# Two transformer blocks on one core: TensorE operands at chosen byte offsets

## Chip, cores and metric

The kernel runs on one core of a Trainium2 chip. The metric is the device time of one execution in microseconds (us); lower is better. Before the change the median of 3 runs is 2297.12 us (2294.67 to 2298.26).

## The reference

256 tokens of width 1024 pass through two blocks, all in float32. What matters here is the chain of matrix products:

```
first_block, 2 layers:  proj = rmsnorm(x) @ w_in            # 1024 -> queries, keys, values, gates
                        three attention branches -> ya, yb, yc
                        merged = sum_b sigmoid(m_g[b]) * (y_b @ w_br_b)
                        x = x + merged @ w_out
second_block, 2 layers (a latent and a context sequence, 256 tokens each):
    x, ctx = half_ffn(x), half_ffn(ctx)     # (silu(h @ w_gate) * (h @ w_up)) @ w_down, 1024 -> 2816 -> 1024
    layer 0: Fourier mixing of both, @ four_w       layer 1: retention, 4 heads, of the latent reading ctx
    x = half_ffn(x); in layer 0 also ctx = half_ffn(ctx)
return rmsnorm(x)
```

## The kernel before

Every product is made exact enough for float32 by splitting each operand into a rounded part and a rest (`wh` and `wl` for weights; `hh`/`ho`, `ah`/`ao`, `xh`/`xo`, `yh`/`yo`, `mh`/`mo`, `gh`/`go`, `qh`/`qo`, `kh`/`ko`, `vh`/`vo`, `Sh`/`So`, `zh`/`zo`, `dh`/`dl` for the rest) and adding three matmuls, in `mm3` (L489 to L491) or written out. A matmul here has a stationary operand of 128 columns, loaded by an instruction of its own, and a moving operand of 256, 384, 452 or 512 columns; both are float32 and lie in SBUF, so a slice of 512 columns takes 2048 bytes of a partition.

The weights come in one long stream. `Stream` loads tiles of up to 2048 columns (`raw`, 3 buffers), and ACT (L388) and DVE (L389) split them into `wh` and `wl`, 4 buffers of 4096 bytes each. The order of all work is written out by hand, and side work (attention, sums for the modulation, norms) is put between the matmuls by `th.tick()`.

The stages, in order, with the operands that matter:

- `layer(0)`, `layer(1)`: projections with `wh`/`wl` moving (512, 452, 384 columns) and `xh`/`xo` stationary (L640 to L642); gates with `xh`/`xo` moving (256); branch products with `wh`/`wl` moving and `yh`/`yo` stationary (L1186 to L1188); the output product with `mh`/`mo` moving (256).
- `ffn(0,0)`, `ffn(0,2)`, `ffn(1,0)` work on both sequences at once (`lanes` 2): gate and up products with `hh`/`ho` moving (512), down products with `ah`/`ao` moving (512). The first two column blocks of gate and up (`start`) and the last two of down (`tail`) go one sequence at a time, with 256 columns.
- `fourier()` between the first two: two transforms with `dh`/`dl` moving (256) and `hh`/`ho`, then `zh`/`zo` stationary, then a product with `hh`/`ho` moving (256).
- `retention()`: per head `rq` (`hh` moving, 256), `rk` (`hh` moving, 512), `rv` and `rg` (`wh`/`wl` moving, 512, `hh`/`ho` stationary, L1598 to L1600), attention (`Sh`/`So` stationary, `vh`/`vo` moving, 512; `kh`/`ko` stationary, `qh`/`qo` moving, 256), and at the end `ro` (`gh`/`go` moving, 256).
- `ffn(1,2)` works on the latent alone (`lanes` 1): `hh`/`ho` and `ah`/`ao` moving, 256 columns.

Where a tile lies follows from its pool. Pools are stacked; within one, tiles lie one behind the other in the order in which they are asked for, each with its size rounded up to 32 bytes. Most pools grow from the lower end. The pools `b2` (`hh`, `ho`, `ss2`, `Rb`, ..., `r4`, `r1`, and small buffers) and `xc` grow downward from the upper end, so that a larger tile in `b2` moves all tiles of `b2` that were asked for before it, and `xc`, to lower addresses. `wh`, `wl`, `xh`, `xo`, `yh`, `yo`, `dh`, `dl` begin at multiples of 256 bytes. Slices of 512 bytes (128 columns), 1024 and 2048 bytes keep a tile's offset within 256 bytes, so that one number describes all slices of a tile.

Of the kernel before, what the change touches and what calls it, by code (L numbers as in the profile page):

```python
# [21 lines left out]
F32 = mybir.dt.float32  # L22
F32R = mybir.dt.float32r
# [7 lines left out]
D, T, KB = 1024, 256, 8  # L31
# [4 lines left out]
RAW, UNIT = 2048, 1024  # L36


# ---------------------------------------------------------------- order of the weights

def xs_items(key, n):
    return [(key, 4 * n, [(0, 2 * n), (2 * n, 4 * n)])] * 2
# [106 lines left out]
    }  # L149


# ---------------------------------------------------------------- layout on the host

def qk_columns():
    def heads(n, ids):
# [170 lines left out]
            "dft": dft_tab(), "decay": decay_tab()}  # L326


# ---------------------------------------------------------------- the program

class Stream:
    AHEAD = 2
# [113 lines left out]
def build(tc, aps, stage=99):  # L446
    nc = tc.nc
    pe, act, dve, pool = nc.tensor, nc.scalar, nc.vector, nc.gpsimd
    from contextlib import ExitStack
    ctx = ExitStack()  # L450
    with ctx:
# [38 lines left out]
            pe.matmul(out, wh, xlo, start=False, stop=False)  # L490
            pe.matmul(out, wl, xh, start=False, stop=last)  # L491

        # ---- adaLN
        def on_ada(key, item):
            _, l, i, n = key
            th.spawn(ada_sum(l, i, n, item))
# [95 lines left out]
                dve.scalar_tensor_tensor(sc[:, :, 0:2], ct.rearrange(kc, c=2), 1.0, ch.rearrange(kc, c=2),  # L592
                                         op0=OP.add, op1=OP.mult)

        # ================================================================ first block
        FB = ctx.enter_context(ExitStack())
        fp = FB.enter_context(tc.tile_pool(name="fb", bufs=1, reuse_waits="tile"))
        xh = fp.tile([128, KB, T], F32R, name="xh")
# [48 lines left out]
        Z = {}  # L647
# [81 lines left out]
        def open_second():  # L729
            ctx.enter_context(B2)  # L730
            ctx.enter_context(XC)
            bp = Z["bp"] = B2.enter_context(tc.tile_pool(name="b2", bufs=1, side=OTHER_SIDE, reuse_waits="tile"))
            xcp = XC.enter_context(tc.tile_pool(name="xc", bufs=1, side=OTHER_SIDE, reuse_waits="tile"))
            xc = xcp.tile([128, KB, T], F32, name="xc")
            nc.scalar.dma_start(xc.rearrange("p k t -> p (k t)"), aps["ctxt"])
            Z["x"] = [xl, xc]
            Z["hh"] = bp.tile([128, KB, 512], F32R, name="hh")
            Z["ho"] = bp.tile([128, KB, 512], F32R, name="ho")
            Z["ss"] = bp.tile([128, 512], F32, name="ss2")
            Z["Rb"] = bp.tile([128, 512], F32, name="Rb")  # L740
            Z["ss1"] = bp.tile([128, T], F32, name="ss1", tag="s1")
            Z["sp"] = bp.tile([128, 2, 3, KB, 2], F32, name="sp")
            Z["sp1"] = bp.tile([128, KB], F32, name="sp1")
            Z["gx"] = bp.tile([128, 2, 3, KB, 2], F32, name="gx")
            Z["r"] = bp.tile([128, 4], F32, name="r4")
            Z["r1"] = bp.tile([128, 2], F32, name="r1")
            th.spawn(ctx_thread(), 2)

# [100 lines left out]
        def layer(l):  # L849
# [83 lines left out]
                pe.matmul(out, qk[hb:hb + 64, qs // 2, t * 128:(t + 1) * 128], qk[hb:hb + 64, ks // 2, 0:L],  # L933
                          start=True, stop=True)

            # ---- the index of branch b
            def index_thread():
                while ("qk", 2) not in flags:
                    yield 1
# [34 lines left out]
                    dve.tensor_tensor(outs[t], outs[t], cms[t], op=OP.add)  # L974
                    flags.add(("bm", t))

            # ---- softmax attention, as a chain of jobs
            jobs = []
            for t in range(2):
                m = (mask0 if t == 0 else mask1)(0)  # L980
# [170 lines left out]
            AT.close()  # L1151
            MT = ExitStack()
            mp = MT.enter_context(tc.tile_pool(name=f"mrg{l}", bufs=1, reuse_waits="tile"))
            mg = mp.tile([128, 2, 1024], F32, name="mg")
            mh = mp.tile([128, KB, T], F32R, name="mh")
            mo = mp.tile([128, KB, T], F32R, name="mo")
# [54 lines left out]
            for q in range(2):  # L1211
                ps = [bank("pj") for _ in range(4)]
                for kh in range(2):
                    for u in range(2):
                        wh, wl = W.get(("out", l, q, kh))
                        for i in range(2):
# [5 lines left out]
                            if kh == 1:  # L1222
                                b = 4 * q + m
# [27 lines left out]
        for l in range(2):  # L1251
            layer(l)
        FB.close()

        # ================================================================ second block
        def ffn(l, j, lanes, nxt, first=0, ready=(), on_k=None, first_s=None, post=None):
            N = 256 * lanes
            FF = ExitStack()
            qp = FF.enter_context(tc.tile_pool(name=f"ffn{l}{j}", bufs=1, reuse_waits="tile"))
            hh, ho, gx = Z["hh"], Z["ho"], Z["gx"]  # L1260
            ah = qp.tile([128, 11, N], F32R, name="ah")
            ao = qp.tile([128, 11, N], F32R, name="ao")
# [121 lines left out]
        def dft_open():  # L1384
            dp = DF.enter_context(tc.tile_pool(name="dft", bufs=1, reuse_waits="tile"))
            Z["dh"] = dp.tile([128, 3, 2, 256], F32R, name="dh")
            Z["dl"] = dp.tile([128, 3, 2, 256], F32R, name="dl")
            def parts():
                yield 4
                for i in range(3):  # L1390
                    r = dp.tile([128, 512], F32, name="dr", tag="dr", bufs=1)
                    nc.sync.dma_start(r, aps["dft"][:, i * 512:(i + 1) * 512])
                    yield 3
                    fl = "p b c -> p (b c)"
                    h, l = Z["dh"][:, i].rearrange(fl), Z["dl"][:, i].rearrange(fl)
                    act.copy(h, r)
                    dve.tensor_tensor(l, r, h.bitcast(F32), op=OP.subtract)

                while not state.get("ada03"):
                    yield 1  # L1400
                f8 = dp.tile([128, 2, 2, 4, 2], F32R, name="f8")
                m = mods[:, 0, 24:32, :].rearrange("p (g d) r -> p d g r", d=2)
                for d in range(2):
                    act.copy(f8[:, 0, d], m[:, d])
                    dve.tensor_tensor(f8[:, 1, d], m[:, d], f8[:, 0, d].bitcast(F32), op=OP.subtract)
                yield 2
                ps = bank("at", "pf8")
                i = 0
                for d in range(2):
                    for x, t in ((0, Z["dh"]), (0, Z["dl"]), (1, Z["dh"])):  # L1410
                        pe.matmul(ps[0:8, 0:256], f8[:, x, d].rearrange("p g r -> p (g r)"), t[:, 0, d, :],
                                  start=(i == 0), stop=(i == 5))
                        i += 1
                yield 1
                c8 = dp.tile([8, 256], F32, name="c8")
                act.copy(c8, ps[0:8, 0:256])
                yield 2
                pt = bank("at", "pc8")
                for t in range(2):
                    pe.transpose(pt[:, 8 * t:8 * t + 8], c8[:, t * 128:(t + 1) * 128], ident[0:8, 0:8])  # L1420
                yield 1
                cm = Z["cm"] = dp.tile([128, 2, 4, 2], F32, name="cm")
                for t in range(2):
                    dve.tensor_copy(cm[:, t].rearrange("p g r -> p (g r)"), pt[:, 0:8])
                dve.tensor_copy(cm[0:1, 1].rearrange("p g r -> p (g r)"), pt[0:1, 8:16])

            th.spawn(parts())
# [7 lines left out]
        def fourier():  # L1435
# [1 line left out]
            xs = Z["x"]  # L1437
            FO = ExitStack()
            qp = FO.enter_context(tc.tile_pool(name="four", bufs=1, reuse_waits="tile"))
            pm = qp.tile([128, 2], F32, name="pm")  # L1440
            dve.memset(pm[:, 0:1], 1.0)
            dve.memset(pm[:, 1:2], -1.0)
            dve.memset(pm[0:1, :], 0.0)
            hh, ho = Z["hh"], Z["ho"]
# [3 lines left out]
            for a in range(2):  # L1448
                for g in range(4):
# [11 lines left out]
                    for t in range(2):  # L1461
                        o, r = ps[:, t * 256:(t + 1) * 256], Z["r"][:, 2 * a + t:2 * a + t + 1]
# [79 lines left out]
        def retention():  # L1542
            hh, ho, gx = Z["hh"], Z["ho"], Z["gx"]
# [3 lines left out]
            RC = ExitStack()  # L1547
            G2 = {}
            axl = qp.tile([128, 2, T], F32, name="axl")
            lg = qp.tile([128, 8], F32, name="lg")  # L1550
            nc.scalar.dma_start(axl.rearrange("p a t -> p (a t)"), aps["axial"])
            dve.tensor_scalar(lg, sm("decay"), -1.0, None, op0=OP.mult)
            dve.tensor_tensor(lg, lg, sm("decay"), op=OP.min)
# [50 lines left out]
            def att(h, qh, qo, kh, ko, vh, vo, sg):  # L1604
# [17 lines left out]
                for it in range(2):  # L1622
                    ps = bank("at", "pY")
                    ts = slice(it * 128, (it + 1) * 128)
                    for jt in range(4):
                        pe.matmul(ps, Sh[:, jt, ts], vh[:, jt, :], start=(jt == 0), stop=False)
                        pe.matmul(ps, Sh[:, jt, ts], vo[:, jt, :], start=False, stop=False)
                        pe.matmul(ps, So[:, jt, ts], vh[:, jt, :], start=False, stop=(jt == 3))
                    st = qp.tile([128, 16], F32, name="st", tag="st", bufs=2)
                    dve.bn_stats(st[:, 0:6], ps)  # L1630
                    dve.bn_aggr(st[:, 8:10], st[:, 0:6])
                    dve.tensor_scalar(st[:, 10:11], st[:, 9:10], 1.0, 1e-6, op0=OP.mult, op1=OP.add)
                    pool.tensor_tensor(st[:, 11:12], st[:, 10:11], mhalf[:, 0:1], op=OP.pow)
                    yn = qp.tile([128, 512], F32, name="yn", tag="tm", bufs=3)
                    dve.tensor_scalar(yn, ps, st[:, 8:9], st[:, 11:12], op0=OP.subtract, op1=OP.mult)
                    dve.tensor_tensor(yn, yn, sg[:, it, :], op=OP.mult)
                    yield 2
                    pt = bank("at", "pYt")
                    for b in range(4):
                        pe.transpose(pt[:, b * 128:(b + 1) * 128], yn[:, b * 128:(b + 1) * 128], ident)  # L1640
                    o = (slice(None), slice(4 * h, 4 * h + 4), ts)
                    pv = pt.rearrange("p (b t) -> p b t", t=128)
                    act.copy(G2["h"][o], pv)
                    dve.tensor_tensor(G2["o"][o], pv, G2["h"][o].bitcast(F32), op=OP.subtract)
# [164 lines left out]
```

## Time and profile before

| | |
|---|---|
| median of 3 runs | 2297.12 us |
| span of the profiled execution, first to last instruction | 2290.2 us |
| median less that span | 6.9 us |
| TensorE matmuls | 12576, busy 2254.1 us (98%) |
| TensorE weight loads | busy 1911.1 us (83%) |
| DVE / ACT / POOL busy | 62% / 40% / 8% |

The profile shows one execution. Matmuls overlap in it: the next one starts before the last has ended, so the time that a matmul costs in a dense stretch is the distance from its start to the next start (called its pace here), not its own length. That the pace is steady in a stretch is seen by dividing the time between two starts by the number of matmuls between them.

### The profile page before, as it was taken

To read this page: it belongs to the slowest core of one execution; us is meant where nothing else is said; L and a number is where in the kernel's file an instruction comes from. 1 tells how busy PE (TensorE), PEld (TensorE's weight loads), DVE (VectorE), ACT (ScalarE), POOL (GpSimd) and SP (SyncE) were. 2 spreads that over 40 slices of the span, in tenths; PEclk is the share of its full clock that TensorE was granted. 3 is DMA by queue.
4 is the path that set the end of the run, shared out by engine and by line. 5 is a ranking of instruction groups with operands and counts; after the bars stand their busy time and mean duration, and the time that the engine had idled before them with its cause. 6 is when DMAs were issued, how large, how long until landed. Compare 5 with 4: busy or idle time off the path is not lost.

```text
span 2290.2 us, 30969 instructions
## 1 busy us (share of the span) xinstructions
PE 2254.1 (98%) x12576; PEld 1911.1 (83%) x12576; DVE 1429.2 (62%) x2160; ACT 918.8 (40%) x1453; POOL 178.2 (8%) x204
## 2 busy tenths in 40 slices
PE   8999999999999999999999999999999999999998
PEld 7787887878877777898788778878878888899998
DVE  6776667766667666556666566555555656665554
ACT  5455544556432233455322324332232533335443
POOL 2100111012100000121000003000001100001001
PEclk9999999999999999999999999999999999999999
DMA  6344565444344544222445443334434423344553
GB/s 236 138 139 154 177 234 196 168 160 175 131 175 165 214 164 135 99 74 101 164 168 184 166 149 137 129 130 165 147 123 147 149 106 125 122 169 151 176 195 108
DMA packets 57167, 351.67 MB, mean 154 GB/s; under 512 B 6464, under 2 KB 6976, under 8 KB 23872
## 3 DMA queue, kind: packets, MB, share of 16 engines
q1 hardware_dynamic: 55872, 346.02, 42.6%
q10 hardware_dynamic: 1152, 3.67, 0.4%
q8 instruction: 98, 1.61, 0.3%
q14 instruction: 45, 0.37, 0.0%
HBM read 348.62 MB, written 1.05 MB: 153 GB/s over the span
## 4 chain that ended last, share of the span: by engine, by line
PE 86%; DVE 6%; ACT 3%; issue 3%; DMA 1%; POOL 1%; SPq 0%; DVEq 0%; ACTq 0%; POOLq 0%
PE pj L489 20%; PE pj L490 20%; PE pj L491 20%; PE pj L640 4%; PE pj L641 3%; PE pj L642 3%; DVE wl L389 2%; PE pj L1600 1%; PE pj L1599 1%; PE pj L1598 1%; ACT wh L388 1%; PE psc L933 1%; PE ada L527 1%; PE ppv L1061 1%; DMA raw<-w 1%
## 5 line engine op out<-in xcount | busy, mean ns | idle before, releaser
L389 DVE TENSOR_TENSOR wl<-raw,wh 128x1024 fp32r<-128x1024 f32 (+4 forms) x549 | 621.4, 1144 | 335.1 <-ACT wh L388 333.9
L388 ACT CAST wh<-raw 128x1024 fp32r<-128x1024 f32 (+4 forms) x549 | 520.6, 967 | 232.7 <-DMA raw<-w 149.7
L489 PE MATMUL pj<-hh,wh 128*128 128x512 f32 (+1 forms) x1632 | 573.1, 351 | 2.0 <-ACT hh L722 1.9
L490 PE MATMUL pj<-ho,wh 128*128 128x512 f32 (+1 forms) x1632 | 571.1, 350 | 3.1 <-POOL ho L727 1.6
L491 PE MATMUL pj<-hh,wl 128*128 128x512 f32 (+1 forms) x1632 | 570.0, 349 | 0.8 <-DVE wl L389 0.8
L489 PEld LDWEIGHTS pj<-hh,wh 128*128 128x128 f32 x1632 | 309.3, 189 | 52.2 <-ACT sg L1266 5.0
L490 PEld LDWEIGHTS pj<-ho,wh 128*128 128x128 f32 x1632 | 309.2, 189 | 46.9 <-POOL ho L727 2.8
L491 PEld LDWEIGHTS pj<-hh,wl 128*128 128x128 f32 x1632 | 309.0, 189 | 43.6 <-DVE wl L389 1.1
L516 DVE SCALAR_TENSOR_TENSOR acc<-raw,sc,acc 128x1024 f32<-128x1024 f32 x224 | 278.9, 1286 | 0.0
L489 PE MATMUL pj<-ah,wh 128*128 128x512 f32 (+1 forms) x770 | 269.6, 350 | 0.5 <-ACT wh L388 0.5
L491 PE MATMUL pj<-ah,wl 128*128 128x512 f32 (+1 forms) x770 | 267.8, 348 | 0.5 <-DVE wl L389 0.5
L490 PE MATMUL pj<-ao,wh 128*128 128x512 f32 (+1 forms) x770 | 267.7, 348 | 0.0
L640 PE MATMUL pj<-wh,xh 128*128 128x512 f32 (+2 forms) x480 | 191.0, 398 | 0.4 <-ACT wh L388 0.4
L641 PE MATMUL pj<-wl,xh 128*128 128x512 f32 (+2 forms) x480 | 184.1, 383 | 2.9 <-DVE wl L389 2.9
L642 PE MATMUL pj<-wh,xo 128*128 128x512 f32 (+2 forms) x480 | 183.2, 382 | 0.0
L1272 ACT CAST ah<-av 128x512 fp32r<-128x512 f32 (+1 forms) x88 | 49.9, 567 | 323.2 <-DVE av L1271 323.2
L489 PEld LDWEIGHTS pj<-ah,wh 128*128 128x128 f32 x770 | 145.6, 189 | 25.2 <-ACT wh L388 3.2
L491 PEld LDWEIGHTS pj<-ah,wl 128*128 128x128 f32 x770 | 145.6, 189 | 19.9 <-DVE wl L389 0.7
L490 PEld LDWEIGHTS pj<-ao,wh 128*128 128x128 f32 x770 | 145.7, 189 | 18.6
L1271 DVE TENSOR_TENSOR av<-sg,pj 128x512 f32<-128x512 f32 (+1 forms) x88 | 54.6, 621 | 161.3 <-PE pj L491 146.7
L670 POOL TENSOR_TENSOR ss<-ss,sq 128x256 f32<-128x256 f32 x55 | 48.6, 890 | 1328.9 <-ACT sq L668 1328.7
L1266 ACT ACTIVATE sg<-pj 128x512 f32<-128x512 f32 (+1 forms) x88 | 47.9, 544 | 206.6 <-PE pj L491 206.6
(304 smaller groups left out, 2964.3 us busy)
## 6 DMA issues: line engine op xcount, KB each, us to landing
raw<-w SPq DMA_DIRECT2D x258, 1024.0 KB, 4.8
raw<-w SPq DMA_DIRECT2D x64, 704.0 KB, 4.1
raw<-w SPq DMA_DIRECT2D x16, 768.0 KB, 4.2
de<-decay SPq DMA_DIRECT2D x24, 256.0 KB, 4.3
raw<-w SPq DMA_DIRECT2D x4, 904.0 KB, 4.5
raw<-w SPq DMA_DIRECT2D x6, 512.0 KB, 4.3
mk<-masks ACTq DMA_DIRECT2D x2, 768.0 KB, 5.6
xl<-xt SPq DMA_DIRECT2D x4, 256.0 KB, 5.5
```

The source lines that it names most:

```text
L388: self.nc.scalar.copy(hi[:, d], r[:, o])
L389: (sub or self.nc.vector).tensor_tensor(lo[:, d], r[:, o], hi[:, d].bitcast(F32), op=OP.subtract)
L489: pe.matmul(out, wh, xh, start=first, stop=False)
L490: pe.matmul(out, wh, xlo, start=False, stop=False)
L491: pe.matmul(out, wl, xh, start=False, stop=last)
L516: dve.scalar_tensor_tensor(acc[:, r, :], w, s, acc[:, r, :], op0=OP.mult, op1=OP.add)
L640: pe.matmul(o, xh[:, k, ts], wh[:, s], start=(k == 0), stop=False)
L641: pe.matmul(o, xh[:, k, ts], wl[:, s], start=False, stop=False)
L642: pe.matmul(o, xo[:, k, ts], wh[:, s], start=False, stop=(k == KB - 1))
L670: (dve if k == KB - 2 else pool).tensor_tensor(d, d, q, op=OP.add)
L1271: dve.tensor_tensor(av, sg, pu[:, :N], op=OP.mult)
L1272: act.copy(ah[:, m, :], av)
```

## The change

The change alters sizes of tiles, so that other tiles move, and in one place gives an operand a tile of its own. Nothing that is computed changes. The diff, without lines that only drop comments:

```diff
             Z["gx"] = bp.tile([128, 2, 3, KB, 2], F32, name="gx")
-            Z["r"] = bp.tile([128, 4], F32, name="r4")
+            Z["r"] = bp.tile([128, 36], F32, name="r4")
...
             mp = MT.enter_context(tc.tile_pool(name=f"mrg{l}", bufs=1, reuse_waits="tile"))
+            skew = mp.tile([128, (32, 40)[l]], F32, name="skew")
+            pool.memset(skew, 0.0)
             mg = mp.tile([128, 2, 1024], F32, name="mg")
...
             qp = FF.enter_context(tc.tile_pool(name=f"ffn{l}{j}", bufs=1, reuse_waits="tile"))
+            if lanes == 1:
+                skew = qp.tile([128, 48], F32, name="skew")
+                pool.memset(skew, 0.0)
+                Z["hh"] = qp.tile([128, KB, N], F32R, name="h1")
+                Z["ho"] = qp.tile([128, KB, N], F32R, name="o1")
             hh, ho, gx = Z["hh"], Z["ho"], Z["gx"]
...
-                c8 = dp.tile([8, 256], F32, name="c8")
+                c8 = dp.tile([8, 272], F32, name="c8")[:, :256]
...
             qp = FO.enter_context(tc.tile_pool(name="four", bufs=1, reuse_waits="tile"))
-            pm = qp.tile([128, 2], F32, name="pm")
+            pm = qp.tile([128, 64], F32, name="pm")
...
-            lg = qp.tile([128, 8], F32, name="lg")
+            lg = qp.tile([128, 64], F32, name="lg")[:, :8]
...
-                    st = qp.tile([128, 16], F32, name="st", tag="st", bufs=2)
+                    st = qp.tile([128, 24], F32, name="st", tag="st", bufs=2)
```

What moves, in bytes past a multiple of 256 (before from the program's list of tiles, after by adding the new sizes rounded to 32 bytes):

| operand | place | columns when moving | before | after | by |
|---|---|---|---|---|---|
| `hh`, `ho` | three two-lane ffns, Fourier, retention | 512, 256, or stationary | 128 | 0 | `r4` 16 to 144 bytes |
| `hh`, `ho` (as `h1`, `o1`) | `ffn(1,2)` | 256 | 128 | 192 | own tiles behind `skew`, 192 bytes |
| `ah`, `ao` | `ffn(0,0)` | 512, in the tail 256 | 192 | 0 | `c8` 1024 to 1088 bytes |
| `ah`, `ao` | `ffn(0,2)`, `ffn(1,0)` | 512, in the tail 256 | 0 | 0 | |
| `ah`, `ao` | `ffn(1,2)` | 256 | 0 | 192 | `skew` |
| `zh`, `zo` | Fourier | stationary | 224 | 0 | `c8`, `pm` |
| `qh`, `kh`, `vh`, `Sh` and rests | retention | 256 (`qh`), 512 (`vh`) | 32 | 0 | `lg` |
| `gh`, `go` | retention, `ro` | 256 | 160 | 192 | `lg`, `st` |
| `mh`, `mo` | merge of layer 0 / layer 1 | 256 | 64 | 192 / 224 | `skew`, 128 / 160 bytes |

## Rows read from the trace of the kernel before

**Rows 1.** The page: busy time by engine; granted TensorE clock by slice; the chain by engine.

```profile
PE 2254.1 (98%) x12576; PEld 1911.1 (83%) x12576; DVE 1429.2 (62%) x2160; ACT 918.8 (40%) x1453; POOL 178.2 (8%) x204
...
PEclk9999999999999999999999999999999999999999
...
PE 86%; DVE 6%; ACT 3%; issue 3%; DMA 1%; POOL 1%; SPq 0%; DVEq 0%; ACTq 0%; POOLq 0%
```

**Rows 2.** Groups of instructions by line and shape, TensorE: count | busy us, mean ns.

```profile
L489 PE MATMUL pj<-hh,wh 128*128 128x512 f32 x960 | 380.6, 396 | 0.0
...
L489 PE MATMUL pj<-hh,wh 128*128 128x256 f32 x672 | 192.4, 286 | 2.0 <-ACT hh L722 1.9
...
L489 PE MATMUL pj<-ah,wh 128*128 128x512 f32 x462 | 182.1, 394 | 0.0
...
L1598 PE MATMUL pj<-wh,hh 128*128 128x512 f32 x144 | 57.2, 397 | 0.0
```

**Rows 3.** Timeline, TensorE, gate and up of `ffn(0,2)`: start us, length us, engine, line.

```profile
1060.22 0.39 PE L489 MATMUL pj<-hh,wh 128*128 128x512 f32 x1
...
1099.95 0.40 PE L489 MATMUL pj<-hh,wh 128*128 128x512 f32 x1
```

**Rows 4.** Timeline, TensorE, down product of `ffn(0,2)`.

```profile
1160.17 0.39 PE L489 MATMUL pj<-ah,wh 128*128 128x512 f32 x1
...
1179.00 0.39 PE L491 MATMUL pj<-ah,wl 128*128 128x512 f32 x1
```

**Rows 5.** Timeline, TensorE, down product of `ffn(0,0)`.

```profile
892.73 0.39 PE L489 MATMUL pj<-ah,wh 128*128 128x512 f32 x1
...
912.10 0.40 PE L491 MATMUL pj<-ah,wl 128*128 128x512 f32 x1
```

**Rows 6.** Timeline, TensorE, retention, `rv` of the first head.

```profile
1824.50 0.40 PE L1598 MATMUL pj<-wh,hh 128*128 128x512 f32 x1
...
1846.62 0.40 PE L1600 MATMUL pj<-wh,ho 128*128 128x512 f32 x1
```

**Rows 7.** Timeline, TensorE, branch products of layer 1.

```profile
536.47 0.39 PE L1186 MATMUL pj<-wh,yh 128*128 128x512 f32 x1
...
547.12 0.39 PE L1188 MATMUL pj<-wh,yo 128*128 128x512 f32 x1
```

**Rows 8.** Timeline, TensorE, gate and up of `ffn(1,2)`, second half.

```profile
2189.85 0.28 PE L489 MATMUL pj<-hh,wh 128*128 128x256 f32 x1
...
2211.92 0.28 PE L489 MATMUL pj<-hh,wh 128*128 128x256 f32 x1
```

**Rows 9.** Timeline, TensorE, down product of `ffn(1,2)`, first half.

```profile
2152.84 0.28 PE L489 MATMUL pj<-ah,wh 128*128 128x256 f32 x1
...
2174.91 0.28 PE L490 MATMUL pj<-ao,wh 128*128 128x256 f32 x1
```

**Rows 10.** Timeline, TensorE, tail of `ffn(0,0)`, two stretches.

```profile
941.93 0.28 PE L489 MATMUL pj<-ah,wh 128*128 128x256 f32 x1
...
943.97 0.28 PE L489 MATMUL pj<-ah,wh 128*128 128x256 f32 x1
...
953.21 0.28 PE L489 MATMUL pj<-ah,wh 128*128 128x256 f32 x1
...
958.04 0.28 PE L491 MATMUL pj<-ah,wl 128*128 128x256 f32 x1
```

**Rows 11.** Timeline, TensorE, output product of layer 0.

```profile
261.65 0.28 PE L489 MATMUL pj<-mh,wh 128*128 128x256 f32 x1
...
264.36 0.28 PE L491 MATMUL pj<-mh,wl 128*128 128x256 f32 x1
```

**Rows 12.** Timeline, POOL, merge of layer 0; in brackets the idle time before.

```profile
214.72 3.53 POOL L1199 TENSOR_TENSOR mg<-mg,tm 128x512 f32<-128x512 f32 x2 [89.79 <-DVE tm L1198]
```

**Rows 13.** Timeline, head of `ffn(1,2)`, TensorE and POOL.

```profile
2086.90 0.58 PE L489 MATMUL pj<-hh,wh 128*128 128x256 f32 x1 [1.52 <-ACT hh L722]
...
2087.76 0.99 POOL L727 TENSOR_TENSOR ho<-hu,hh 128x256 fp32r<-128x256 f32 x1 [3.13 <-ACT hh L726]
```

## The prediction

> **What bounds the kernel now.** I read the page first. TensorE is busy 98% of the span, most of the chain that ended last lies on it, and its granted clock is in the top tenth in all 40 slices [rows 1]. So the time is, but for the heads of stages, a sum of matmul paces. The change touches no engine's work, only where operands lie; the question is whether the pace depends on that. The groups by shape give the counts but not the pace, since the listed length of a matmul, 394 to 397 ns for 512 columns, overlaps the next one [rows 2]. So I went to the timeline of TensorE alone, took stretches of one kind, and divided the time between the first and the last start by the number of starts less one.
>
> With 512 columns:
>
> - `hh` moving at offset 128, `wh` stationary at 0: 172 starts in 39.73 us, 232.3 ns [rows 3].
> - `ah` moving at 0, `wh` stationary at 0, same ffn: 84 starts in 18.83 us, 226.9 ns [rows 4].
> - `ah` moving at 192, `wh` at 0: 84 starts in 19.37 us, 233.4 ns [rows 5].
> - `wh` moving at 0, `hh` stationary at 128: 96 starts in 22.12 us, 232.8 ns [rows 6].
> - `wh` moving at 0, `yh` stationary at 0: 48 starts in 10.65 us, 226.6 ns [rows 7].
>
> The reader should see two things. Equal down products go at 226.9 or 233.4 ns and differ in `ah`'s offset. And with `wh` moving at 0 both times, the pace is 226.6 or 232.8 as the stationary operand lies at 0 or 128: it is the pair that counts, and both at a multiple of 256 is the fastest seen.
>
> With 256 columns the order is another one:
>
> - `hh` at 128: 187 starts in 22.07 us, 118.7 ns [rows 8].
> - `ah` at 0: 185 starts in 22.07 us, 119.9 ns, the slowest [rows 9].
> - `ah` at 192: 19 starts in 2.04 us, 113.3 ns; later in the same tail, after a short break for the column sums, 42 starts in 4.83 us, 117.8 ns [rows 10]. The offset is the same in both, so this case has two steady paces, and something like the phase in which a stretch begins picks one.
> - `mh` at 64: 24 starts in 2.71 us, 117.8 ns [rows 11].
>
> **The change part by part.** First the gains at 512 columns, all by a larger tile ahead of the operand.
>
> *`r4`, 128 bytes more:* `hh` and `ho` go from 128 to 0. Gate and up of the three two-lane ffns: 960 matmuls on each of three lines [rows 2], 2880, from 232.3 to 226.9: 5.5 ns each before rounding, 15.8 us. `rk`: 4 heads x 2 blocks x 8 x 3 = 192, 1.0 us. `rv` and the first `rg` are 144 on each of three lines [rows 2], the later `rg` 3 x 2 x 8 x 3 = 144: 576 with `hh` stationary, 232.8 to 226.9 [rows 4, 6], 3.4 us.
>
> *`c8`, 64 bytes more:* `ah`, `ao` of `ffn(0,0)` go from 192 to 0. The 462 on a line are three ffns [rows 2], so one ffn has 154 x 3 = 462, from 233.4 to 226.9 [rows 4, 5]: 3.0 us.
>
> *`lg`:* `vh` and `Sh` go from 32 and 32 to 0 and 0, 2 x 4 x 3 x 4 = 96 matmuls. No row above prices that; bounds are nothing and 96 x 6.5 = 0.6 us; I take 0.2, since the two are already at the same offset.
>
> Sum at 512: 23.4 us.
>
> Then the losses at 256, the other side of the same edits. `hh` at 0 in place of 128: `start` 192 in each of three ffns, Fourier's product 384, `rq` 192, together 1152, from 118.7 to 119.9 [rows 8, 9], 1.5 us. The tail of `ffn(0,0)`: 132 from the middle of 113.3 and 117.8 to 119.9, 0.6 us. The transforms, 204 with `hh`, `zh` stationary at 128 and 224: no row above; between nothing and 2 ns each, I take 0.3 us. Loss 2.4 us.
>
> Then the gains at 256, by `skew`, `h1`, `o1`, `st`. All go to 192, whose pace is 113.3 to 117.8 [rows 10]; I take the middle, 115.5, because the trace shows both and nothing in it says which a new stretch will fall into. Gate and up of `ffn(1,2)`: 22 x 2 x 8 x 3 = 1056 from 118.7: 0.9 to 5.7, taken 3.3. Down: 2 x 8 x 11 x 3 = 528 from 119.9: 1.1 to 3.5, taken 2.3. `gh`, 384 from about 118 (the rows at 64 and 128 stand on both sides): 0.1 to 1.8, taken 1.0. `mh`: 192 in layer 0 from 117.8 to 192's pace, 0 to 0.9; 192 in layer 1 to 224, which no row shows, between -0.4 (119.9) and 0.9 (113.3); taken together 0.6. Gain 7.2 us, bounds 1.7 to 12.8 with all at one end or the other.
>
> Edits that I cost at nothing. The two memsets of layers 0 and 1 run on POOL ahead of the merge; POOL has been idle 89.8 us before its next addition [rows 12]. The one in `ffn(1,2)` stands ahead of the `ho` subtractions, before which POOL is idle 3.1 us [rows 13]. Both also wait for the last reader of the tile that lay there (`rope`, `axl`), long past. Without that cover the last would delay TensorE's start of `ffn(1,2)`, by about one POOL instruction, 1 us [rows 13]. Queued behind it are only those subtractions. `h1` and `o1` lie on tiles of the retention (`axl` to `Dm`), whose last readers belong to the last head's attention, drained before the second half of `ro`; TensorE's wait at that head is for ACT's `hh` as now, 1.5 us [rows 13], and keeps its length. The larger `pm` makes one memset 64 elements long on one partition. No DMA is added or moved, nor any waits in SP's queue.
>
> Sum: -23.4 + 2.4 - 7.2 = -28.2 us. Some may come back where a faster TensorE meets something late: of the chain 14% is not TensorE [rows 1], which bounds it at 4 us; most of that 14% are heads of stages that do not change, so I take 1.2. Net -27 us: span 2290.2 to 2263.2. The median of the runs lies 6.9 us above the profiled span; with that, 2270.1 us.
>
> A rule that speaks against all of this: the Trainium skill, "TensorE: Matmul & The Clock Gate", section on the back-to-back issue gap, gives the distance of two matmuls by their columns and the clock alone, 215.7 ns measured for 512 and 55.6 for 128, with no word on where operands lie. The trace does not agree with that as a whole account: 226.6 to 233.4 ns for the same shape. By the rule the sum would be 0.
>
> **The rivals.**
>
> *Half.* The fast pace is a matter of the stage as well: down products and branch products may be fast because fewer or other accesses of ACT and DVE run beside them, and gate and up would then settle between. For it: offset 192 shows two paces, so offset is not all. Against: rows 6 and 7 differ only in stage and offset, but so do rows 4 and 5, which are one kind of work, and the difference is the same 6 ns. Price: half of 28, 2297.1 - 14 = 2283 us.
>
> *No change.* Offsets do nothing; the paces belong to the stages. Against: rows 4 and 5 again. Time 2297 us, 2294 to 2300. The Trainium skill says as much: "SBUF — State Buffer", section "Who interferes with whom", gives TensorE one read port for the moving operand and an independent one for the weights, and lets TensorE wait for nobody. No row here shows ports; the paces by offset speak against the conclusion.
>
> *Slower.* At 512 columns, what holds for 256 also holds for `hh`: both at 0 is the slowest pair (119.9 against 118.7), because two reads then begin in step. Place: gate and up, `rk`, `rv`, `rg`, 2880 + 192 + 576 = 3648 matmuls. Price: 1.2 ns per 256 columns is 2.4 per matmul, 8.8 us; with 3.0 more in `ffn(0,0)`, its gain turned into as large a loss, and 2.4 - 7.2 at 256, +7.0, 2304 us. It decides once gate and up go slower than about 233.6 ns (4.8 us of net gain at 256 over 3648 matmuls is 1.3 ns). Against: `ah` at 0 and `yh` at 0 are just this pair and fast [rows 4, 7].
>
> **How the numbers follow.** Forecast 0.80, half 0.10, no change 0.05, slower 0.05. The forecast's own range, with the 256-column bounds and 0 to 4 us given back, is -33.8 to -18.7: 2263 to 2278 us. To hold 8 in 10 I take one more us below and reach up to the half case: 2262 to 2284. About 0.2% (4.6 us) is what a measurement here can tell from no change. Faster by more 0.90 (forecast and half), within it 0.05, slower by more 0.05.
>
> **What would show it.** Timeline paces after: gate and up of the two-lane ffns near 227; `rv` near 227; down of `ffn(0,0)` near 227; `ffn(1,2)` between 113 and 118 in gate, up and down, perhaps changing after a break; Fourier's product and `rq` near 120. The prediction is wrong if gate and up stay above 230 with both operands at 0, if the 256-column matmuls at 192 go over 119, or if TensorE's idle time at stage heads grows by more than 4 us.

## The result and the profile after

The changed kernel takes 2267.11 us (median of 4: 2263.74, 2264.06, 2270.17, 2271.37), the kernel before on the same chip 2296.6 (2294.67 to 2298.26): ratio 0.9875, 95% interval 0.9857 to 0.9893. That is 29.5 us or 1.25% less; forecast were 27.0 us less and 2270.1 us.

The profiled execution is the one of 2270.17 us. Its page, as in [rows 1], and its groups by line and shape, as in [rows 2]:

```profile
span 2268.4 us, 30969 instructions
...
PE 2231.9 (98%) x12576; PEld 1907.8 (84%) x12576; DVE 1428.7 (63%) x2160; ACT 919.4 (41%) x1453; POOL 179.2 (8%) x207
...
PE 87%; DVE 5%; ACT 3%; issue 2%; DMA 1%; POOL 1%; SPq 0%; DVEq 0%; ACTq 0%; POOLq 0%
```

```profile
L489 PE MATMUL pj<-hh,wh 128*128 128x512 f32 x960 | 375.6, 391 | 0.0
...
L489 PE MATMUL pj<-ah,wh 128*128 128x512 f32 x462 | 181.3, 392 | 0.0
...
L1605 PE MATMUL pj<-wh,hh 128*128 128x512 f32 x144 | 57.3, 398 | 0.0
```

The span fell by 21.8 us and TensorE's busy time by 22.2 (2254.1 to 2231.9), with the same 12576 matmuls: no engine waits less, the same work is denser. The groups by shape hardly tell: 396 to 391 ns for gate and up, 397 to 398 for `rv`. The pace is in the timeline. TensorE after, first and last start of a stretch: down of `ffn(0,0)` [rows 5], Fourier's product, gate and up of `ffn(0,2)` [rows 3], `rv` [rows 6], and of `ffn(1,2)` down [rows 9] and gate and up [rows 8]:

```profile
699.84 0.39 PE L489 MATMUL pj<-ah,wh 128*128 128x512 f32 x1
...
711.17 0.39 PE L491 MATMUL pj<-ah,wl 128*128 128x512 f32 x1
...
999.57 0.28 PE L489 MATMUL pj<-hh,wh 128*128 128x256 f32 x1
...
1020.33 0.28 PE L491 MATMUL pj<-hh,wl 128*128 128x256 f32 x1
...
1060.13 0.39 PE L489 MATMUL pj<-hh,wh 128*128 128x512 f32 x1
...
1099.58 0.39 PE L489 MATMUL pj<-hh,wh 128*128 128x512 f32 x1
...
1810.01 0.39 PE L1605 MATMUL pj<-wh,hh 128*128 128x512 f32 x1
...
1831.54 0.39 PE L1607 MATMUL pj<-wh,ho 128*128 128x512 f32 x1
...
2132.25 0.28 PE L489 MATMUL pj<-ah,wh 128*128 128x256 f32 x1
...
2152.98 0.28 PE L491 MATMUL pj<-ah,wl 128*128 128x256 f32 x1
...
2199.74 0.28 PE L489 MATMUL pj<-h,wh 128*128 128x256 f32 x1
...
2221.88 0.28 PE L491 MATMUL pj<-h,wl 128*128 128x256 f32 x1
```

| stretch | starts | us | ns after | ns before |
|---|---|---|---|---|
| gate and up, `ffn(0,2)` | 175 | 39.45 | 226.7 | 232.3 |
| down, `ffn(0,0)` | 51 | 11.33 | 226.6 | 233.4 |
| `rv` | 96 | 21.53 | 226.6 | 232.8 |
| Fourier's product | 174 | 20.76 | 120.0 | |
| down, `ffn(1,2)` | 177 | 20.73 | 117.8 | 119.9 |
| gate and up, `ffn(1,2)` | 189 | 22.14 | 117.8 | 118.7 |

Where the time came from is read from busy time by stretch, with the stages as bounds (layer 1; `ffn(0,0)`; Fourier's product to the end of `ffn(1,0)`; retention; `ffn(1,2)` and the norm). Columns: length, busy time and count of each engine, TensorE's granted clock, DMA share, GB/s.

```profile
285.00:572.50 287.50, 283.42 (x1680) 233.03 (x1679) 196.59 (x404) 151.70 (x267) 47.83 (x54) 0.99 0.52 186
572.50:952.40 379.90, 377.85 (x1858) 312.66 (x1857) 250.44 (x309) 128.30 (x188) 14.77 (x20) 1.00 0.46 160
...
977.60:1776.60 799.00, 795.68 (x4050) 669.26 (x4049) 473.73 (x566) 265.37 (x396) 52.10 (x58) 1.00 0.41 144
1776.60:2060.90 284.30, 281.75 (x1580) 245.86 (x1579) 179.42 (x275) 116.55 (x167) 13.89 (x21) 0.99 0.40 141
2060.90:2268.40 207.50, 192.43 (x1607) 191.34 (x1605) 116.76 (x159) 93.20 (x145) 11.14 (x14) 0.96 0.46 159
```

Before, the same five, columns as above:

```profile
285.30:571.30 286.00, 281.80 (x1681) 232.04 (x1680) 196.39 (x403) 151.28 (x267) 47.89 (x53) 1.00 0.51 187
571.30:958.20 386.90, 384.65 (x1858) 312.57 (x1857) 250.27 (x309) 128.25 (x188) 14.67 (x20) 1.00 0.45 158
...
983.10:1792.10 809.00, 806.05 (x4049) 670.69 (x4049) 473.83 (x566) 265.18 (x396) 52.11 (x58) 1.00 0.40 142
1792.10:2080.20 288.10, 285.59 (x1579) 246.07 (x1578) 179.68 (x275) 116.29 (x167) 13.87 (x21) 1.00 0.39 140
2080.20:2290.20 210.00, 195.11 (x1607) 193.86 (x1605) 116.69 (x159) 93.16 (x145) 11.10 (x13) 0.96 0.45 156
```

So +1.5, -7.0, -10.0, -3.8 and -2.5; layer 0 gave -0.3 and the transforms +0.3. The sum is -21.8.

### The profile page after: what moved, and what is told of

Read it like the earlier page. It is cut to its first block, busy times and chain, and to the rows that moved or that the text cites. A ratio compares the mean times of both kernels' runs of the same rounds, so it can differ in the third digit from the quotient of the medians.

```text
span 2268.4 us, 30969 instructions
## 1 busy us (share of the span) xinstructions
PE 2231.9 (98%) x12576; PEld 1907.8 (84%) x12576; DVE 1428.7 (63%) x2160; ACT 919.4 (41%) x1453; POOL 179.2 (8%) x207
## 3 DMA queue, kind: packets, MB, share of 16 engines
q10 hardware_dynamic: 1152, 3.67, 0.5%
## 4 chain that ended last, share of the span: by engine, by line
PE 87%; DVE 5%; ACT 3%; issue 2%; DMA 1%; POOL 1%; SPq 0%; DVEq 0%; ACTq 0%; POOLq 0%
PE pj L489 20%; PE pj L490 20%; PE pj L491 20%; PE pj L640 4%; PE pj L641 3%; PE pj L642 3%; DVE wl L389 2%; PE pj L1605 1%; PE pj L1607 1%; PE pj L1606 1%; ACT wh L388 1%; PE psc L933 1%; PE ada L527 1%; PE ppv L1061 1%; DMA raw<-w 1%
## 5 line engine op out<-in xcount | busy, mean ns | idle before, releaser
L490 PE MATMUL pj<-ho,wh 128*128 128x512 f32 (+1 forms) x1280 | 465.6, 364 | 3.4 <-POOL ho L727 1.8
L489 PE MATMUL pj<-hh,wh 128*128 128x512 f32 (+1 forms) x1280 | 467.4, 365 | 0.5 <-ACT hh L722 0.4
L491 PE MATMUL pj<-hh,wl 128*128 128x512 f32 (+1 forms) x1280 | 464.3, 363 | 0.8 <-DVE wl L389 0.8
L489 PEld LDWEIGHTS pj<-hh,wh 128*128 128x128 f32 x1280 | 241.4, 189 | 45.6 <-ACT sg L1273 5.0
L490 PEld LDWEIGHTS pj<-ho,wh 128*128 128x128 f32 x1280 | 241.5, 189 | 42.8 <-POOL ho L727 3.4
L491 PEld LDWEIGHTS pj<-hh,wl 128*128 128x128 f32 x1280 | 241.5, 189 | 39.2 <-DVE wl L389 1.0
```

What stands on the lines that cost most here:

```text
L489: pe.matmul(out, wh, xh, start=first, stop=False)
```

## The experiments

Two theories stood against each other: the difference of the two offsets sets the pace (A), or the stage does (C). A third was that only operands at multiples of 256 bytes are fast (B).

**A sweep with nothing else running.** A kernel of its own: matmuls on resident operands, two blocks of 24 between breaks, for 512 and 256 columns.

```diff
+PAIRS = [(m, 0) for m in range(0, 256, 16)] + [(m, 128) for m in range(0, 256, 32)] + \
+        [(m, 64) for m in range(0, 256, 32)]
...
+                a, b = s // 4 + k * 128, m // 4 + (k % 4) * 512
+                x, y = hh[:, b:b + n], ho[:, b:b + n]
+                pe.matmul(o, wh[:, a:a + 128], x, start=(k == 0), stop=False)
```

> A kernel of its own that computes nothing of the reference: resident operands, stretches of 48 matmuls of 512 and of 256 columns, in threes as in mm3, for 32 pairs of offsets of the moving and the stationary operand within 256 bytes, each pair twice, with four two-column float32 matmuls ahead of each stretch; then four stretches of 96 at moving 192, stationary 0. Theory A (only the difference moving less stationary counts): the same pace for the same difference whether the stationary operand lies at 0, 64 or 128; at 512 columns 227 ns at difference 0 and 232 to 234 at 128 and 192; at 256 columns 120 at 0, 118 at 64, 118 to 119 at 128, and 113.3 or 117.8 at 192. Theory B (it counts that both lie at a multiple of 256): 227 ns at 512 columns only for 0 and 0, and 230 or more for 64 and 64 or 128 and 128. Theory C (the stage, not the offset): one pace for each width, 227 and 120, at every offset, since nothing else runs.

The timeline, 24 intervals each: 512 columns with moving and stationary at 0 and 0, 128 and 0, 128 and 128; then 256 columns at 112 and 0, and at 192 and 0 twice.

```profile
36.66 0.39 PE L52 MATMUL pj<-hh,wl 128*128 128x512 f32 x1
...
42.10 0.40 PE L52 MATMUL pj<-hh,wl 128*128 128x512 f32 x1
...
221.34 0.39 PE L52 MATMUL pj<-hh,wl 128*128 128x512 f32 x1
...
226.91 0.40 PE L52 MATMUL pj<-hh,wl 128*128 128x512 f32 x1
...
500.58 0.39 PE L52 MATMUL pj<-hh,wl 128*128 128x512 f32 x1
...
506.02 0.39 PE L52 MATMUL pj<-hh,wl 128*128 128x512 f32 x1
...
861.66 0.28 PE L52 MATMUL pj<-hh,wl 128*128 128x256 f32 x1
...
864.38 0.28 PE L52 MATMUL pj<-hh,wl 128*128 128x256 f32 x1
...
922.61 0.28 PE L52 MATMUL pj<-hh,wl 128*128 128x256 f32 x1
...
925.33 0.28 PE L52 MATMUL pj<-hh,wl 128*128 128x256 f32 x1
...
928.60 0.28 PE L52 MATMUL pj<-hh,wl 128*128 128x256 f32 x1
...
931.42 0.28 PE L52 MATMUL pj<-hh,wl 128*128 128x256 f32 x1
```

5.44, 5.57, 5.44, 2.72, 2.72 and 2.82 us over 24: 226.7, 232.1, 226.7, 113.3, 113.3 and, from the unrounded starts, 117.8 ns. A holds without any other engine at work, so C falls; 128 and 128 is as fast as 0 and 0, so B falls. For a stationary operand at 0, 64 or 128 only the difference, moving less stationary modulo 256, counts:

| difference | 512 columns, ns | 256 columns, ns |
|---|---|---|
| 0 | 226.7 | 120.0 |
| 64 | 228.9 | 117.8 |
| 112 | 226.7 or 231.1 | 113.3 |
| 128 | 232.1 | 118.5 |
| 192 | 233.3 | 113.3 or 117.8 |
| the other multiples of 16 | 230.0 to 236.7 | 116.7 to 120.0 |

The Trainium skill, "SBUF — State Buffer", section "Who interferes with whom", gives TensorE independent read ports for the moving operand and the weights and says that it never waits on anyone. As a whole account this does not agree with these rows: 232.1 against 226.7 ns with no other engine at work. The rows show that the two operands of one matmul matter to each other, not by which port.

**More differences and widths.** The same kernel with differences that lie 8 bytes past a multiple of 16, entries of other lengths, and 384 and 452 columns.

```diff
+        for m in list(range(8, 256, 16)) + [100, 108, 116, 124]:
...
+        for m in (112, 192):
...
+        for n in (384, 452):
```

> A second kernel of its own that computes nothing of the reference: 256 columns at differences of 8 bytes past multiples of 16 and near 112; differences 112 and 192 entered after one to eight two-column float32 matmuls and after a stretch of 512 columns; 384 and 452 columns at differences on a grid of 32. Theory A2: 112 gives 113.3 ns at every entry, 192 gives 113.3 at some and 117.8 at others; 384 columns at 0 near 173 ns. Rival: 112 shows both paces as well.

At 256 columns, 112 gave 113.3 in 12 of 12 entries, 192 in 4 of 12 (7 of 22 with the first sweep): in 4 of the 8 entered after short matmuls and in none of the 4 entered after 512 columns. The differences off a multiple of 16 stayed at 116.7 to 122.8. With 384 columns 173.3 ns at 0, 64, 112, 160, 192 and 224, 175.6 at 128, 176.7 at 32 and 96; with 452 columns 203.3 at 160, 204.5 at 112, 205.6 at 64 and 206.7 at the others.

**Both at 128.** In the kernel before, one tile ahead of the weights moves `wh` and `wl` to 128, where `hh` lies.

```diff
         sc = P.tile([128, KB, 32], F32, name="sc")
+        pad = P.tile([128, 32], F32, name="pad")
+        dve.memset(pad, 0.0)
```

> The kernel before with one unused tile of 128 bytes ahead of the weights' buffers and all pools that grow from the lower end, and its memset. wh, wl, xh, yh and ah of two ffns go from 0 to 128, hh and ho stay at 128. No operand lies at a multiple of 256 any more, and hh and wh have the same offset. Theory A (the difference counts): gate and up of the two-lane ffns, rk, rv and rg at 227 ns, all others as before; about -20 us there, +3 us for the 256-column matmuls of hh, 2280 us. Theory B (multiples of 256): gate and up stay at 232, the down products of two ffns and the projections go up to 232, about +13 us, 2310 us.

2275.67 us against 2295.1, ratio 0.992 (0.9905 to 0.9935). Gate and up of `ffn(0,2)`, 175 starts:

```profile
1060.22 0.39 PE L491 MATMUL pj<-hh,wh 128*128 128x512 f32 x1
...
1099.66 0.39 PE L491 MATMUL pj<-hh,wh 128*128 128x512 f32 x1
```

39.44 us, 226.7 ns, in the real kernel with `hh` unmoved: the pair, not the place, and about two thirds of the whole change from one tile of 128 bytes.

**`r4` alone.**

```diff
-            Z["r"] = bp.tile([128, 4], F32, name="r4")
+            Z["r"] = bp.tile([128, 36], F32, name="r4")
```

> The kernel before with the larger r4 alone: hh and ho from 128 to 0, nothing else moved. By the paces: 2880 + 192 + 576 matmuls of 512 columns 5.5 to 6 ns faster (-20 us), 2208 of 256 columns 1.3 ns slower (+3 us): 2279 us, and gate and up at 227 ns, the last ffn's at 120. Rival (the other edits of the change are what saves, or the saving needs all of them): within 5 us of the kernel before.

2278.0 us, ratio 0.9928 (0.9913 to 0.9942): as expected within 1 us.

**`r4` to the wrong place.** The same tile 32 bytes larger, which takes `hh` to 96.

```diff
-            Z["r"] = bp.tile([128, 4], F32, name="r4")
+            Z["r"] = bp.tile([128, 12], F32, name="r4")
```

> The kernel before with r4 larger by 32 bytes, so that hh and ho lie at 96 in place of 128. Theory A, by the sweep's paces: 3072 matmuls of 512 columns from 232.4 to 233.3 (+2.8 us), 576 with hh stationary (difference 160) from 232.3 to 234.2 (+1.1), 2208 of 256 columns from 118.7 to 120.0 (+2.9): 6.8 us slower, 2302 us. Rival (only 0 is special, all other offsets are alike): no change, 2295 us.

2299.86 us against 2295.96, ratio 1.0018 (1.0009 to 1.0028). Gate and up, 173 starts in 40.14 us:

```profile
1069.70 0.40 PE L490 MATMUL pj<-ho,wh 128*128 128x512 f32 x1
...
1109.84 0.39 PE L491 MATMUL pj<-hh,wl 128*128 128x512 f32 x1
```

233.4 ns, the sweep's 233.3. The sign is right and the size 3.9 of 6.8 us; in the two traces the three kinds of matmuls that were named cost 2.1, 0.9 and 2.6 us more, some 5.7 together, and the kernel before scatters by 6.5 us from one execution to the next. A larger tile as such wins nothing.

**The changed kernel again.** No edit, three profiles, to see what 192 does from one execution to the next.

> The changed kernel once more, five times. Its first four times lie in two groups, 2263.7 and 2264.1, and 2270.2 and 2271.4. Theory A2 (the last ffn's 1584 matmuls with their moving operand at 192 keep either 113.3 or 117.8 ns throughout): again two groups, 7.0 us apart (1584 x 4.4 ns), nothing between them, and in the profile the last ffn at 113.3 if the run is of the faster group, at 117.8 if of the slower. Rival (ordinary scatter, or the head's waits): times spread over 2263 to 2272, and the last ffn at 117.8 in any profile.

> The changed kernel, one look: theory A2 says that the time lies near 2263 or near 2270, and that the last ffn stands at 113.3 ns in the profile in the first case, at 117.8 in the second. Rival (the groups have another cause): 117.8 in both.

> The changed kernel, a second look, as the first: near 2263 with the last ffn at 113.3 ns, or near 2270 with 117.8.

The first took 2269.24 us in the profiled execution and 2265.68, 2262.08 and 2264.14 in others (median 2264.91, ratio 0.9866, 0.9849 to 0.9882); the second 2268.92, the third 2264.09. In the third, gate and up to down of `ffn(1,2)`, 196 starts:

```profile
2199.80 0.28 PE L491 MATMUL pj<-h,wl 128*128 128x256 f32 x1
...
2221.90 0.28 PE L491 MATMUL pj<-ah,wl 128*128 128x256 f32 x1
```

22.10 us, 113.3 ns; in the two others 117.8, as in the table above. The same program has both paces, and the last that it falls into holds to the end of that ffn: from its first to its last start 182.5 us against 189.1 in the second. With the two rounds of times together, the ten executions lie at 2262.1 to 2265.7 (six) and 2268.9 to 2271.4 (four); of the four with a trace, the one of the lower group has 113.3 and the three of the upper 117.8.

The moment at which the pace drops can be seen in the profile after, TensorE and its weight loads:

```profile
2076.07 0.28 PE L489 MATMUL pj<-h,wh 128*128 128x256 f32 x1
2076.07 0.19 PEld L490 LDWEIGHTS pj<-o,wh 128*128 128x128 f32 x1
...
2076.18 0.28 PE L490 MATMUL pj<-o,wh 128*128 128x256 f32 x1
2076.20 0.19 PEld L491 LDWEIGHTS pj<-h,wl 128*128 128x128 f32 x1
...
2076.30 0.28 PE L491 MATMUL pj<-h,wl 128*128 128x256 f32 x1
...
2076.42 0.28 PE L489 MATMUL pj<-h,wh 128*128 128x256 f32 x1
```

Up to there a load starts 3 or 4 ns behind the matmul before it and the distance is 0.11; then one load comes 12 ns behind (0.02 us as rounded here), and from there on the distance is 0.12 to the end of the ffn. The loads after it come 2 to 5 ns behind again. The first of the three further profiles shows the same: at 2074.1 us two loads come 172 and 107 ns behind, with 113.3 before them and 117.8 after. In the second the pace is 117.8 from the first dense stretch on. That late loads cause the drop was not tried by an experiment, and what made these late is open.

**112 in place of 192.** By the sweep, 112 has one pace only. In the changed kernel `h1`, `o1`, `ah`, `ao`, `mh`, `mo`, `gh`, `go` go to 112, and `zh`, `zo` (stationary) to 144, for instance:

```diff
-                skew = qp.tile([128, 48], F32, name="skew")
+                skew = qp.tile([128, 24], F32, name="skew")
...
-                Z["hh"] = qp.tile([128, KB, N], F32R, name="h1")
+                Z["hh"] = qp.tile([128, KB * N + 64], F32R, name="h1")[:, 4:4 + KB * N].rearrange("p (k t) -> p k t", t=N)
```

> The changed kernel with all that it puts at 192 or 224 put at 112: h1, o1, ah and ao of the last ffn, mh, mo, gh, go; and zh, zo at 144, so that dh less zh is 112 too. In the sweep a difference of 112 gave 113.3 ns both times at 256 columns, 192 gave 113.3 or 117.8. Theory A2 (112 has the fast pace alone): the last ffn at 113.3 throughout, 1584 x 4.4 = 7.0 us under the slower group of the changed kernel, mh of layer 1, gh and zh some 2 us more: 2261 us, all times in one group. Rival (112 has the slow pace too, and which one a stretch keeps is chance): two groups, about 2262 and 2269, or all at 2269.

2262.84 us (2261.7 to 2263.66, one group), ratio 0.9858 (0.9843 to 0.9873). `ffn(1,2)`, 197 starts:

```profile
2199.78 0.28 PE L489 MATMUL pj<-h,wh 128*128 128x256 f32 x1
...
2222.00 0.28 PE L490 MATMUL pj<-ao,wh 128*128 128x256 f32 x1
```

22.22 us, 113.4 ns. It is the lowest time measured, and it has no upper group; its interval overlaps that of the changed kernel. The transforms, with `zh` stationary at 144, went at 118.4 and not at 113.3.

**The last ffn taken out of the change, and the last ffn alone.**

```diff
-            if lanes == 1:
-                skew = qp.tile([128, 48], F32, name="skew")
-                pool.memset(skew, 0.0)
-                Z["hh"] = qp.tile([128, KB, N], F32R, name="h1")
-                Z["ho"] = qp.tile([128, KB, N], F32R, name="o1")
```

> The changed kernel without its edit in the last ffn: no skew, h1 and o1 there, so that hh, ho, ah and ao all lie at 0. Theory: 1584 matmuls of 256 columns at 120.0 ns in place of 117.8 or 113.3, 3.5 us over the slower group or 10.5 over the faster: 2274 us, all times in one group. Rival (the two groups come from elsewhere, such as the head of the last ffn or the retention): two groups as before.

2273.82 us (2272.32 to 2274.16, one group), ratio 0.9905 (0.989 to 0.992), and `ffn(1,2)` goes at 120.0 ns.

The other is the kernel before with these five lines alone.

> The kernel before with the edit of the last ffn alone (skew, h1, o1: 192 for hh, ho, ah, ao there). Theory A2: 1056 matmuls from 118.7 and 528 from 120.0 to 117.8 or to 113.3: 2.2 us or 9.2 us under the kernel before, two groups, 2293.5 and 2286.5. Rival (the edit does nothing of its own, its gain needs the other edits): 2295.6.

Seven executions: 2284.05 to 2289.06 (five), 2294.38 and 2296.53; median 2286.6, ratio 0.9966 (0.9954 to 0.9978). The profiled execution is that of 2296.53, and its `ffn(1,2)` goes at 117.8 ns throughout, 1.8 us less than in the kernel before. Expected were 2293.5 and 2286.5; the upper two lie among the times of the kernel before (2292.67 to 2297.28), and in the one with a trace 1.5 us were lost in `rv` and `rg`, where the clock fell (below). So the two groups are seen with these lines and not without them; no trace shows whether `ffn(1,2)` goes at 113.3 in the lower one here too, and the single group without the lines rests on four executions.

**112 in the tails, by way of the weights.** From the 112 version, the weights of the tails of the two-lane ffns are written 144 bytes into their tiles, so that the difference is 112 with `ah` at 0.

```diff
+            key = self.items[i][0]
+            if key[0] == "dn" and key[3] == 1 and key[4] > 5 and key[1:3] != (1, 2):
+                hi, lo = hi[:, 36:36 + c1 - c0], lo[:, 36:36 + c1 - c0]
```

> The kernel with 112 in place of 192, and the last two column blocks of the down product of the three two-lane ffns with their weights written 144 bytes into wh and wl, so that ah less wh is 112 there too. Theory A: 396 matmuls of 256 columns from 120.0 to 113.3, 2.6 us: 2260.2 us, and the tails at 113.3 in the profile. Rival (the tails wait for their sums, so that a faster pace is given back): 2262.8.

A miss: 2264.5 us (2263.65 to 2265.16), ratio 0.9866 (0.9853 to 0.9879), and a tail goes at 119.8 ns (81 starts in 9.58 us). With `zh` at 144 this is the second place where a stationary operand at 144 does not follow the difference. So that rule is shown for stationary operands at 0, 64 and 128 alone; for which others it holds is open.

## Why the prediction was right

The distances from start to start, summed over all matmuls of a kind, before against after:

| term | forecast, us | measured, us |
|---|---|---|
| `hh` moving, 512: gate, up, `rk` (3072) | -16.8 | -17.4 |
| `rv`, `rg` (576) | -3.4 | -1.3 |
| `ah` of `ffn(0,0)`, 512 | -3.0 | -2.4 |
| `vh` | -0.2 | -0.1 |
| `hh` moving, 256 (1152) | +1.5 | +1.35 |
| tail of `ffn(0,0)` (132) | +0.6 | +0.4 |
| `gh` | -1.0 | -1.3 |
| `mh` | -0.6 | -0.3 |
| transforms | +0.3 | +0.35 |
| `ffn(1,2)` | -5.6 | -2.3 here, -8.9 in the execution at 113.3 |

- *"It is the pair that counts, and both at a multiple of 256 is the fastest seen."* The first half is shown, by the sweep and by the tile that moves the weights. The second was too narrow: at 512 columns equal offsets are fast wherever they were tried (0, 64 and 128).
- *The gains at 512 and the losses at 256* came to within 0.6 us each, but for one. In `rv` and `rg` the undisturbed matmuls, those less than 300 ns apart, give 3.1 us (on average 232.5 ns before, 227.2 after); some 1.8 came back, 1.4 of it in seven matmuls at a lower clock. Busy time by stretch after, and then the same place before, columns as above:

```profile
1787.00:1790.00 3.00, 1.26 (x6) 1.07 (x7) 1.51 (x5) 2.13 (x4) 1.39 (x2) 0.93 0.21 87
1790.00:1793.00 3.00, 3.00 (x8) 2.32 (x8) 2.31 (x5) 1.78 (x4) 0.45 (x1) 0.50 0.36 104
```

```profile
1803.00:1806.00 3.00, 1.77 (x9) 1.52 (x10) 1.51 (x3) 2.10 (x4) 1.38 (x2) 1.00 0.05 19
```

After a wait of 1.84 us for POOL's `r`, the granted clock is 0.50 (the 1.2 GHz level), and seven matmuls go at 427 ns. Before, after a wait of 1.81 us at the same place, it stayed at 1.00. All seven profiles of the changed kernel and of variants made from it have this dip, and of the five of the kernel before and of versions made from it one; whether the change makes it likelier is open. That one is the version with the last ffn's lines alone, so the dip also comes without the rest of the change. With `r4` alone there is no dip, and `rv` and `rg` gain 2.9 us. Layer 1, too, shows 0.99 for 1.00, and one dip of five matmuls more than before: some 0.9 of its 1.5 us. That dip is also in the four profiles of versions made from the kernel before, so it is not the change's. Some 3.3 us came back in these two places, where 1.2, at most 4, were forecast, and the larger part (1.4 and 0.9) came back through the clock and not through a late operand.
- *"The middle, 115.5, because the trace shows both and nothing in it says which a new stretch will fall into."* This is the term that was mis-sized most. The middle is what no execution does: `ffn(1,2)` has 117.8 (gain 2.3) or 113.3 (gain 8.9), and the executions lie in two groups some 6 us apart. Bounds of 2.0 to 9.2 for the two terms were right; the value taken, 5.6, fell between the two.
- *The edits costed at nothing*: TensorE starts `ffn(1,2)` 6.5 us after the end of `ro` (2060.9 to 2067.4), before 6.7 [rows 13]. The memsets, `h1` and `o1` cost nothing.
- *"The median of the runs lies 6.9 us above the profiled span."* After, the profiled execution's own time is 1.8 us above its span, and so it is in every other execution with both. So some 5 of the 6.9 were scatter between the executions of the kernel before, which took 2292.1 to 2298.8 us. That, and the profiled execution's place in the upper group, is why the span fell by 21.8 and the median by 29.5. So it is in part luck that the medians differ by 29.5 where 27.0 were forecast: the four executions fell two and two into the groups, and the comparison of the two profiles alone gives 21.8, that with the execution at 113.3 27.9.
- *The rivals.* Half: fell, gate and up go at 226.7 without any other engine and in the kernel alike. No change: fell with it. Slower by equal offsets: fell; what it feared is there at 256 columns (120.0 at difference 0, among the slowest) and not at 512. Whether two reads begin in step is shown by no run.

What is left: why 112 and 192 at 256 columns and not others, what chooses the pace at 192, and whether the 256-column matmuls that still go at 120 (the Fourier product, `start`, `rq`, the tails) can be brought to 113.3 in place.

## What to carry to other kernels

Where TensorE is dense, read the pace from start to start, not from the listed length, and compare equal shapes by where their operands lie. With 512 float32 columns, put the moving and the stationary operand at equal offsets modulo 256 bytes; a smaller width wants another difference (112 for 256 columns here), which a sweep on resident operands finds in one run. When a trace shows two paces for one shape at one offset, forecast two times and not their mean, and look for an offset that has one.

## What the runs showed of the hardware

- The distance of two equal matmuls depends on the difference of their operands' offsets: 226.7 to 236.7 ns for 512 columns, 113.3 to 122.8 for 256, with nothing else running (stationary operand at 0, 64 or 128). The Trainium skill, "TensorE: Matmul & The Clock Gate", section "Wait — 56ns, not 53.3ns?", gives 215.7 ns from start to start for 512 columns at the full clock; no stretch here reached it, the lowest being 226.6.
- The best difference at 512 columns, 0 (226.7 ns), is among the worst at 256 (120.0 ns, where 112 has 113.3).
- At 192 a stretch of 256 columns keeps 113.3 or 117.8 ns for over 180 us, and in both changes of pace seen it went from the one to the other behind a late weight load (12 ns after its matmul in one, 172 ns in the other), where the loads before it started 3 or 4 ns after theirs; whether the load is the cause is open.
